# Gated values of two heads in units of one token tile by 512 columns, in a hybrid decoder trunk

## The chip, the cores and the metric

The kernel runs as one program on one core of a Trainium2 chip. The metric is the time of one execution in microseconds of device time; lower is better. Before the change the median of three runs is 835.55 us (834.86 to 836.42 us).

## The reference, cut to what matters

One layer of a decoder works on 512 tokens of width 1024. After an RMS norm, one projection `h @ w_in` with 11352 columns makes the inputs of three branches: chunked gated linear attention (GLA, 4 heads), sparse attention with a top-k indexer (DSA, 8 query heads) and cross-attention into 256 memory tokens. Each branch is gated, projected and merged, and a last projection and norm close the layer. The change touches the GLA values `gv`: 1024 of the 11352 columns, 256 for each of four heads.

```python
h = rmsnorm(x, g_pre[i])
(gq, gk, gv, ga, gz, dq, dk, dv, iq, ik, iw, dz, xq, xz, gates) = split_cols(h @ w_in[i])
...
att = jnp.einsum('bnthd,bnshd->bnhts', q_d, k_d)
att = jnp.where(causal, att, jnp.zeros_like(att))
o_intra = jnp.einsum('bnhts,bnshv->bnthv', att, v)
def step(state, inp):
    qc, kc, vc, dc = inp
    o = jnp.einsum('bthd,bhdv->bthv', qc, state)
    state = dc[..., None] * state + jnp.einsum('bthd,bthv->bhdv', kc, vc)
    return state, o
...
o = o_intra + o_inter.transpose(1, 0, 2, 3, 4)
o = rmsnorm(o.reshape(B, L, H, dv), g_head)
return o.reshape(B, L, H * dv) * jax.nn.silu(z)
```

## The kernel before, in words

Every product of two float32 matrices is made of three matmuls on a high and a low part of each operand: high by high, high by low, low by high (`mm3`, lines 106 to 109). The high part is a copy by ACT that rounds (`high`, line 94), the low part what is left, taken by DVE (`low`, lines 98 and 100).

Weights come from memory in loads of 1 MB, two chunks in each, into two buffers (`load_next`, L130). A chunk of 1024 columns on 128 partitions is split into its parts `whi` and `wlo` (`split_next`), which have four buffers each. The high part is issued at once; the low part is put on the list `late` and issued by `flush`, which runs behind the matmuls of the next quarter. When the last chunk of a load is split, the next load is issued on SP's queue.

The work is a list of units, in an order written out by hand. A unit is an accumulator of 128 by 512 in PSUM (tag `mm`, two buffers), filled in four quarters by 24 or 48 matmuls and then evicted by its `done`. Unit u needs chunk u (a pair of value units shares two chunks). In the main loop (from line 1103) each quarter's matmuls are issued, then `flush`, then `need`, which splits chunks up to an index ahead of time, then `done` after the fourth quarter, and then whatever `at(name, s, ...)` has hung on this slot. Slots count on beyond a unit's own four: `at("gz1.0", 11, ...)` runs eleven quarters after the first of `gz1.0`. Every engine works through its own instructions in this order.

The units begin with `dv` (0 and 1, in an opening of their own), `pc` (2), `gv0.0`, `gv0.1`, `gv1.0`, `gv1.1` (3 to 6), `iq0` and `iq1` (7 to 10), and then for each GLA head `gqk` (two units), for heads 2 and 3 `gv` (two units), and `gz` (two). In this order `gqk2` are units 19 and 20 and `gv2` units 21 and 22.

A `gv` unit (`unit_n`) takes two token tiles of 128 tokens by one head's 256 columns: the tokens are the stationary operand, the weights the moving one, in 48 matmuls of 256 columns. The values of heads 0 and 1 are made from the input before its norm is known (`g_lhs`), so their eviction multiplies by `rstd`, one 256-column piece at a time (`gv_done`); those of heads 2 and 3 use the normalised input and are evicted in one piece of 512.

On the slots behind `pc` hang the steps that finish the norm (`h_norm`, nine of them), `gate_operands`, the evictions of the four `dv` accumulators (`dv_done`) and the gates' logarithms (`gate_log`). On those behind `gz` hang attention, state, output, norm and result of each GLA head (`gla_att`, `gla_turn_k`, `gla_state`, `gla_out`, `gla_norm`, `gla_y`) and sixteen rounds of top-k (`topk_max`, `topk_drop`), which begin at `gz1.0`.

Of the kernel before, what the change touches and what calls it, by code (L numbers as in the profile page):

```python
# [11 lines left out]
F32R = mybir.dt.float32r  # L12
# [8 lines left out]
KT = 8  # L21
# [4 lines left out]
OFF = {}  # L26
# [15 lines left out]
    _pair(f"iq{_i}", OFF["iq"] + 256 * _i, OFF["iq"] + 256 * _i + 128)  # L42
for _h in range(4):
    _pair(f"gqk{_h}", OFF["gq"] + 128 * _h, OFF["gk"] + 128 * _h)
    for _n in ("gv", "gz", "dq", "dz", "xq", "xz"):
        _pair(f"{_n}{_h}", OFF[_n] + 256 * _h, OFF[_n] + 256 * _h + 128)
_pair("dk", OFF["dk"], OFF["dk"] + 128)
_pair("dv", OFF["dv"], OFF["dv"] + 128)
for _b in range(3):
    for _j in range(4):  # L50
        _c = OFF["gates"] + 1024 * _b + 256 * _j
        _pair(f"gate{_b}{_j}", _c, _c + 128)
NORMAL = ("gv", "dv")
PIDX = {n: i for i, (n, _, _) in enumerate(PAIRS)}


@with_exitstack
def trunk(ctx, tc, x, x_t, mem, w_in, w_c, w_kv, w_out, w_o, cols, g_mem, g_post, w_up, toe, out):
    nc = tc.nc
    pe, act, dve, pool, sp = nc.tensor, nc.scalar, nc.vector, nc.gpsimd, nc.sync  # L60

# [19 lines left out]
    def w4(name, dt=F32, n=1024):  # L81
        return wk.tile([128, n], dt, name=name, tag="w4", bufs=6)
# [19 lines left out]
    def split(hi, lo, src, scale=1.0):  # L102
        high(hi, src, scale)
        low(lo, src, hi, scale)

    def mm3(o, lh, ll, rh, rl, first=True, last=True):
        pe.matmul(o, lh, rh, start=first, stop=False)  # L107
        pe.matmul(o, lh, rl, start=False, stop=False)  # L108
        pe.matmul(o, ll, rh, start=False, stop=last)  # L109


    chunks, loads = [], []
# [54 lines left out]
    units, slots = [], {}  # L167
    where = {}

    def unit(name, quarter, done):  # L170
        where[name] = len(units)
        units.append((quarter, done))

    def at(name, s, fn, *a):
        slots.setdefault(4 * where[name] + s, []).append((fn, a))
# [16 lines left out]
    def unit_n(name, first, lhs, tiles, done):  # L192

        o = []

        def quarter(q):
            if q == 0:
                o.append(psum("mm", name))
            n = len(tiles)
            for i in range(2 * n * q, 2 * n * q + 2 * n):  # L200
                j, k = divmod(i, KT)
                wh, wl = chunks[first + k // 4][3]
                ah, al = lhs(k, tiles[j])
                mm3(o[0][:, 256 * j:256 * j + 256], ah, al, wh[:, k % 4], wl[:, k % 4],
                    k == 0, k == KT - 1)

        unit(name, quarter, lambda: done(o[0]))

    hh = keep.tile([128, KT, T], F32R, name="hh", tag="hh")
    hl = keep.tile([128, KT, T], F32R, name="hl", tag="hl")  # L210
# [23 lines left out]
    def win_n(name, done, lhs=h_lhs):  # L234
        add_chunks(w_in[PIDX[name]], True)
        first = len(units)
        for i in range(2):
            unit_n(f"{name}.{i}", first, lhs, (2 * i, 2 * i + 1), lambda p, i=i: done(i, p))
# [61 lines left out]
    R = {}  # L300

    def dv_done(tt, p):
        if tt == 0:
            R["dvh"], R["dvl"] = kv4("dvh", [4, 256], F32R), kv4("dvl", [4, 256], F32R)
        split(R["dvh"][:, tt], R["dvl"][:, tt], p[:, :256], R["rstd"][:, tt:tt + 1])
# [66 lines left out]

    GV = {}

    def gv_done(h, i, p):
        if i == 0:
            GV[h] = [w4(n, F32R).rearrange("p (t d) -> p t d", t=4) for n in ("vh", "vl")]
        vh, vl = GV[h]
        if h < 2:
            for j in range(2):  # L380
                tt = 2 * i + j
                split(vh[:, tt], vl[:, tt], p[:, 256 * j:256 * j + 256], R["rstd"][:, tt:tt + 1])
            return
        split(vh[:, 2 * i:2 * i + 2], vl[:, 2 * i:2 * i + 2], p.rearrange("p (t d) -> p t d", t=2))

    for h in range(2):
        win_n(f"gv{h}", lambda i, p, h=h: gv_done(h, i, p), g_lhs)


    def gate_log(h):  # L390
# [23 lines left out]

    at("pc", 0, rstd_row)
    for tt in range(4):
        at("gv1.0", tt, lambda tt=tt: dv_done(tt, R["dvps"][tt]))
    for k in range(9):
        at("pc", 1 + k, h_norm, k)

# [13 lines left out]

    for i in range(2):
        win_t(f"iq{i}", iq_done, n=384, rhs=lambda k: (hh[:, k, 128:512], hl[:, k, 128:512]))
    at("gv0.1", 2, gate_operands)
    at("iq0.1", 2, turn_iw)
    for h in range(4):
        at("gv1.1", h, gate_log, h)  # L440
    at("iq0.0", 3, gate_ln, 0)
    at("iq0.1", 0, gate_ln, 1)

# [157 lines left out]

    def gla_state(h, p):
        g = G[h]
        vh, vl = GV[h]
        kv = psum("at", "kv")
        mm3(kv[:, :256], g["kkh"][:, 128 * p:128 * p + 128], g["kkl"][:, 128 * p:128 * p + 128],
            vh[:, p], vl[:, p])
        S = w2("S", n=256)
        if p == 0:
            act.activation(S, kv[:, :256], AF.Copy)  # L610
        else:
            dve.scalar_tensor_tensor(S, g["Sp"], g["pd"][:, p:p + 1], kv[:, :256],
                                     op0=OP.mult, op1=OP.add)
        sh = w2("Sh", F32R)
        split(sh[:, 0:256], sh[:, 256:512], S)
        g["Sp"] = S
        g["S"].append(sh)

    def gla_out(h, i):
        g = G[h]  # L620
        vh, vl = GV[h]
        if i == 0:
            g["on"] = w4("on")
        on = g["on"]
        po = psum("at", "po")
        ss = s8("gss", 2)
        for j in range(2):
            p = 2 * i + j
            o = po[:, 256 * j:256 * j + 256]
            mm3(o, g["ah"][:, p], g["al"][:, p], vh[:, p], vl[:, p], True, p == 0)  # L630
            if p:
                s, sh = slice(128 * p - 128, 128 * p), g["S"][p]
                mm3(o, g["q2h"][:, s], g["q2l"][:, s], sh[:, 0:256], sh[:, 256:512], False, True)
        for j in range(2):
            p = 2 * i + j
            act.activation(on[:, 256 * p:256 * p + 256], po[:, 256 * j:256 * j + 256],
                           AF.Square, scale=1.0 / 16, accum_out=ss[:, j:j + 1])
        v = s8("gvar", 2)
        pool.tensor_scalar(v, ss, EPS, None, op0=OP.add)
        g["r", i] = po, rstd_of(v, 2)  # L640
# [18 lines left out]

    for h in range(4):  # L660
        win_t(f"gqk{h}", lambda i, p, h=h: (gla_q, gla_k)[i](h, p))
        if h > 1:
            win_n(f"gv{h}", lambda i, p, h=h: gv_done(h, i, p))
        z_units(f"gz{h}")


# [317 lines left out]
    def split_b(i):  # L984
        split_next([w[:, i].rearrange("p (k m) -> p k m", m=512) for w in F["w"]])


    for i in range(24):
        at("gqk0.0", 2+i, score, 1 + i // 8, i % 8)
# [4 lines left out]
        at(f"gz{h - 1}.1", 0, gla_exps, h)  # L994
    for h in range(4):
        z = f"gz{h}"
        if h < 2:
            at(z + ".0", h, gla_att, h, 0)
            at(z + ".0", h + 1, gla_att, h, 1)
            at(z + ".0", h + 2, gla_turn_k, h)  # L1000
            for p in range(3):
                at(z + ".1", 2*p + h, gla_state, h, p)
            after = 6 + h
        else:
            v = f"gv{h}"
            at(v + ".1", 0, gla_att, h, 0)
            at(v + ".1", 1, gla_att, h, 1)
            at(v + ".1", 2, gla_turn_k, h)
            for p in range(3):
                at(z + ".0", 2+p, gla_state, h, p)  # L1010
            after = 2
        for i in range(2):
            at(z + ".1", after + 2 * i, gla_out, h, i)
            at(z + ".1", after + 2 * i + 1, gla_norm, h, i)
            at(z + ".1", after + 10 + 2 * i, gla_y, h, i)
# [35 lines left out]
    with tc.manual_schedule():  # L1051
# [3 lines left out]
        loads[0][2] = wdv  # L1055
        state["load"] = 1
        act.dma_start(col, cols)
        for k in range(2):
            act.dma_start(R["xt"][0][:, k], x_t[:, k])
        for k in range(4):  # L1060
            h, c = k // 2, slice(512 * (k % 2), 512 * (k % 2) + 512)
            sp.dma_start(wdv[:, h, c], loads[0][0][:, h, c])
            if k:
                sp.dma_start(R["xt"][k], x_t[:, 2 * k:2 * k + 2])
        for tt in range(4):
            sp.dma_start(xs[tt], x[128 * tt:128 * tt + 128])
            if tt == 1:
                load_next()
# [34 lines left out]
        for u in range(2, len(units)):  # L1103
            quarter, done = units[u]
            for s in range(4):
                quarter(s)
                flush()
                if s == 1 and u < wo_first:
                    need(u + 2)
                if s == 3 and u + 2 < wo_first and chunks[u + 2][2]:  # L1110
                    need(u + 3)
                if s == 2 and u == wo_first - 1 or s == 0 and u == wo_first:
                    need(u + 3, True)
                if s == 3:
                    done()
                for fn, a in slots.pop(4 * u + s, []):
                    fn(*a)
# [12 lines left out]
def _layout(inputs):  # L1130
# [20 lines left out]
    wc[:, 64:80] = w[:, OFF["ga"]:OFF["ga"] + 16]  # L1151
    wc[:, 80:88] = w[:, OFF["iw"]:OFF["iw"] + 8]
    wc[:, 96:112] = wc[:, 64:80]
    a["w_c"] = pairs(wc, [(0,)])[0]
    four = [(256 * j, 256 * j + 128) for j in range(4)]
    wkv = np.asarray(inputs["w_mem_kv"])[0]
# [34 lines left out]
```

## Time and profile before

| | before |
|---|---|
| median of three runs | 835.55 us |
| the profiled execution's own time | 835.18 us |
| its span | 833.5 us |
| PE busy | 818.7 us, 98% |
| DVE busy | 473.8 us, 57% |
| ACT busy | 337.1 us, 40% |
| GpSimd busy | 50.2 us, 6% |
| HBM over the span | 101 GB/s |

Times inside the profile count from the start of the span, and the profiled execution takes 1.7 us more than its span. PE is TensorE's matmuls, DVE is VectorE, ACT is ScalarE, POOL is GpSimd and SP the engine whose queue issues most transfers. A matmul's duration contains its way through the array; successive ones overlap, so their cost is read from start to start. `Lnn` is a line of the kernel; `high`, `low` and `mm3` are helpers, so lines 94, 98, 100 and 107 to 109 are told apart by the tiles that they write. In square brackets a row may say how long the engine stood idle before the instruction and what ended that.

### The profile page before, as it was taken

The numbers are of one execution on the slowest core, as the hardware profiler recorded it, in microseconds if no ns is written. First come the engines' busy times: TensorE is split into PE (matmuls) and PEld (weight loads), VectorE is DVE, ScalarE is ACT, GpSimd is POOL, SyncE is SP. The second block draws the span as 40 slices with busy tenths as digits, with TensorE's granted clock in tenths as the row PEclk, the third lists the DMA queues.
The fourth block names the chain that finished last, engine by engine and source line by source line (L and its number), as shares of the span: only waits on it lengthen the run. The fifth ranks groups of instructions, "written<-read, shape, count | busy, mean of one in ns | idle before, by whom it ended". The sixth has DMA issues, their size and how long they took to land.

```text
span 833.5 us, 10783 instructions
## 1 busy us (share of the span) xinstructions
PE 818.7 (98%) x4320; PEld 704.3 (85%) x4320; DVE 473.8 (57%) x850; ACT 337.1 (40%) x608; POOL 50.2 (6%) x74
## 2 busy tenths in 40 slices
PE   7989999999999999999999999999999999999997
PEld 7989888989888888888888888889989898888885
DVE  4759677888686435446676543545655554343623
ACT  6577554453423223334444422334434343322320
POOL 1000010010000030032131000000000000000000
PEclk9999999999999999999999999999999999999999
DMA  9324121121222231222131125323324142226402
GB/s 332 117 102 138 51 91 62 52 101 53 100 101 101 101 105 73 101 104 99 51 108 71 51 101 176 101 101 101 112 92 147 56 152 70 86 98 223 156 1 102
DMA packets 16387, 86.30 MB, mean 104 GB/s; under 512 B 2064, under 2 KB 2576, under 8 KB 7760
## 3 DMA queue, kind: packets, MB, share of 16 engines
q1 hardware_dynamic: 15328, 84.02, 28.6%
q10 hardware_dynamic: 1008, 1.58, 0.5%
q8 instruction: 34, 0.56, 0.3%
q14 instruction: 17, 0.14, 0.0%
HBM read 82.42 MB, written 2.10 MB: 101 GB/s over the span
## 4 chain that ended last, share of the span: by engine, by line
PE 86%; DVE 5%; ACT 4%; DMA 2%; issue 2%; ACTq 0%; SPq 0%; DVEq 0%; POOLq 0%; POOL 0%
PE out L109 5%; PE out L107 5%; PE out L108 5%; PE pfin L109 2%; PE pfin L108 2%; PE pfin L107 2%; DVE wlo L98 1%; DMA x<-x 1%; PE tpp L721 1%; ACT whi L94 1%; DMA xt<-x_t 1%; PE pov L108 1%; PE pov L109 1%; PE lg L109 1%; PE lg L108 1%
## 5 line engine op out<-in xcount | busy, mean ns | idle before, releaser
L98 DVE TENSOR_TENSOR wlo<-wraw,whi 128x1024 fp32r<-128x1024 f32 (+1 forms) x135 | 163.4, 1211 | 84.4 <-ACT whi L94 83.5
L94 ACT ACTIVATE whi<-wraw 128x1024 fp32r<-128x1024 f32 (+1 forms) x135 | 139.4, 1039 | 22.2 <-PE out L108 19.6
L107 PE MATMUL out<-yh,whi 128*128 128x512 f32 x192 | 75.3, 392 | 0.0
L109 PE MATMUL out<-yh,wlo 128*128 128x512 f32 x192 | 74.8, 390 | 0.0
L108 PE MATMUL out<-yl,whi 128*128 128x512 f32 x192 | 74.8, 389 | 0.0
L707 ACT ACTIVATE bm<-bm,nm 128x128 f32<-128x128 f32 (+3 forms) x32 | 18.0, 564 | 73.6 <-DVE nm L705 71.8
L691 POOL TENSOR_TENSOR bm<-toe,madd 128x128 f32<-128x128 f32 (+3 forms) x32 | 31.0, 986 | 194.6 <-DMA toe<-toe 86.3
L109 PEld LDWEIGHTS out<-yh,wlo 128*128 128x128 f32 x192 | 36.0, 188 | 7.5
L107 PEld LDWEIGHTS out<-yh,whi 128*128 128x128 f32 x192 | 36.1, 188 | 7.3
L108 PEld LDWEIGHTS out<-yl,whi 128*128 128x128 f32 x192 | 36.1, 188 | 7.2
L94 ACT ACTIVATE yh<-th 128x512 fp32r<-128x512 f32 x16 | 10.1, 632 | 44.0 <-DVE th L657 24.9
L512 DVE SCALAR_TENSOR_TENSOR gth<-gth,out 128x512 f32<-128x512 f32 x16 | 11.0, 686 | 28.0 <-PE out L109 28.0
L273 POOL TENSOR_TENSOR rstd<-var,mhalf 128x1 f32<-128x1 f32 x6 | 3.3, 550 | 374.9 <-DVE var L952 289.7
L470 DVE MATCH_REPLACE8 madd<-m,madd 128x256 f32<-128x256 f32 (+2 forms) x48 | 25.6, 543 | 0.0
L466 DVE MAX8 m<-madd 128x8 f32<-128x256 f32 (+2 forms) x48 | 23.6, 546 | 0.0
L705 DVE CUSTOM_DVE_ANT_0 bm<-lg,bm 128x128 f32<-128x128 f32 (+3 forms) x32 | 15.5, 486 | 12.9 <-PE lg L109 12.7
L751 DVE TENSOR_TENSOR ydsa<-pov,th 128x128 f32<-128x128 f32 x32 | 7.8, 286 | 22.5 <-PE pov L109 22.1
L94 ACT ACTIVATE pth<-tpp 128x128 fp32r<-128x128 f32 (+3 forms) x32 | 13.7, 428 | 13.4 <-PE tpp L721 13.4
L456 DVE SCALAR_TENSOR_TENSOR madd<-relu,iw,madd 128x256 f32<-128x256 f32 (+2 forms) x21 | 12.9, 616 | 9.2 <-ACT relu L452 8.9
L949 ACT ACTIVATE sq<-pfin 128x512 f32<-128x512 f32 x8 | 4.8, 598 | 31.5 <-PE pfin L109 31.5
L98 DVE TENSOR_TENSOR yl<-th,yh 128x512 fp32r<-128x512 f32 x16 | 11.1, 693 | 11.2 <-ACT yh L94 11.2
L98 DVE TENSOR_TENSOR ptl<-tpp,pth 128x128 fp32r<-128x128 f32 (+3 forms) x32 | 15.5, 484 | 0.0
(1024 smaller groups left out, 2359.1 us busy)
## 6 DMA issues: line engine op xcount, KB each, us to landing
wraw<-w_in SPq DMA_DIRECT2D x43, 1024.0 KB, 4.8
wraw<-w_out SPq DMA_DIRECT2D x12, 1024.0 KB, 4.8
wraw<-w_kv SPq DMA_DIRECT2D x8, 1024.0 KB, 4.8
wraw<-w_o SPq DMA_DIRECT2D x4, 1024.0 KB, 4.8
x<-x SPq DMA_DIRECT2D x4, 512.0 KB, 8.2
toe<-toe SPq DMA_DIRECT2D x8, 256.0 KB, 5.2
xres<-x SPq DMA_DIRECT2D x4, 512.0 KB, 8.5
xt<-x_t SPq DMA_DIRECT2D x3, 512.0 KB, 7.6
```

The lines of the kernel that those rows point to most:

```text
L94: act.activation(hi, src, AF.Copy, scale=scale)
L98: dve.tensor_tensor(lo, src, f(hi), op=OP.subtract)
L107: pe.matmul(o, lh, rh, start=first, stop=False)
L108: pe.matmul(o, lh, rl, start=False, stop=False)
L109: pe.matmul(o, ll, rh, start=False, stop=last)
L456: dve.scalar_tensor_tensor(sc, r[:, :n], iw[:, b, h:h + 1], sc, op0=OP.mult, op1=OP.add)
L466: dve.max(out=M8[b], in_=maskadd[b])
L470: dve.match_replace(out=maskadd[b], in_to_replace=M8[b], in_values=maskadd[b], imm_value=-FMAX)
L512: dve.scalar_tensor_tensor(th, th, 1.0, p, op0=OP.add, op1=OP.mult)
L691: pool.tensor_tensor(bm[:, :n], Q[hp]["toe"][i][:, 384 - 128 * qb:512], maskadd[qb], op=OP.add)
L705: dve.tensor_tensor_reduce(out=bm[:, :n], in0=lg[:, :n], in1=bm[:, :n], scale=-1.0, scalar=FMAX, op0=OP.add, op1=OP.min, accum_out=nm)
L707: act.activation(bm[:, :n], bm[:, :n], AF.Exp, scale=-1.0, bias=nm, accum_out=su)
```

## The change

The four pairs of value units become two groups of four wide units, `gvw0` (heads 0 and 1, units 3 to 6) and `gvw1` (heads 2 and 3, units 21 to 24). A wide unit (`wide_units`) takes one token tile by 512 columns, which are two heads, in 24 matmuls; quarter q uses the group's chunk q, so each unit of a group uses all four chunks. The weights have a layout of their own, `w_gv`. The value tiles hold two token tiles by 512 columns; `gv_of` cuts out a head's part.

The order of splits is now `ahead`: in front of a group, chunk f+1 is split in the second and f+2 in the fourth quarter of unit f-1, and f+3 behind the first quarter of unit f; no further chunk is split until the group's last unit, which orders the next two. With head 3 losing its own value units, its GLA steps hang on `gz3` as those of heads 0 and 1 do. In the opening, one transfer of `x_t` goes from ACT's queue to SP's, behind the first piece of `wdv`; `dv_done` and `gate_operands` move to slots in `gvw0.2` and `gvw0.3`.

```diff
-    for _n in ("gv", "gz", "dq", "dz", "xq", "xz"):
+    for _n in ("gz", "dq", "dz", "xq", "xz"):
...
+    wide = set()
+
+    def wide_units(name, src, lhs, done):
+
+        first = len(units)
+        wide.add(first)
+        for i in range(2):
+            add_chunks(src[i], None)
+        for tt in range(4):
+            o = []
+
+            def quarter(q, tt=tt, o=o):
+                if q == 0:
+                    o.append(psum("mm", name))
+                wh, wl = chunks[first + q][3]
+                for k in (2 * q, 2 * q + 1):
+                    ah, al = lhs(k, tt)
+                    mm3(o[0], ah, al, wh[:, k % 2], wl[:, k % 2], k == 0, k == KT - 1)
+
+            unit(f"{name}.{tt}", quarter, lambda tt=tt, o=o: done(tt, o[0]))
...
-    def gv_done(h, i, p):
-        if i == 0:
-            GV[h] = [w4(n, F32R).rearrange("p (t d) -> p t d", t=4) for n in ("vh", "vl")]
-        vh, vl = GV[h]
-        if h < 2:
-            for j in range(2):
-                tt = 2 * i + j
-                split(vh[:, tt], vl[:, tt], p[:, 256 * j:256 * j + 256], R["rstd"][:, tt:tt + 1])
-            return
-        split(vh[:, 2 * i:2 * i + 2], vl[:, 2 * i:2 * i + 2], p.rearrange("p (t d) -> p t d", t=2))
-
-    for h in range(2):
-        win_n(f"gv{h}", lambda i, p, h=h: gv_done(h, i, p), g_lhs)
+    def gv_done(g, tt, p):
+        if tt == 0:
+            GV[g] = [[w4(n, F32R).rearrange("p (t d) -> p t d", t=2) for n in ("vh", "vl")]
+                     for _ in range(2)]
+        vh, vl = GV[g][tt // 2]
+        split(vh[:, tt % 2], vl[:, tt % 2], p, 1.0 if g else R["rstd"][:, tt:tt + 1])
+
+    def gv_of(h, p):
+        return [t[:, p % 2, 256 * (h % 2):256 * (h % 2) + 256] for t in GV[h // 2][p // 2]]
+
+    wide_units("gvw0", [w_gv[0], w_gv[1]], g_lhs, lambda tt, p: gv_done(0, tt, p))
...
-        at("gv1.0", tt, lambda tt=tt: dv_done(tt, R["dvps"][tt]))
+        at("gvw0.2", 1 + tt, lambda tt=tt: dv_done(tt, R["dvps"][tt]))
...
-    at("gv0.1", 2, gate_operands)
+    at("gvw0.2", 0, gate_operands)
...
-        at("gv1.1", h, gate_log, h)
+        at("gvw0.3", h, gate_log, h)
...
-        if h > 1:
-            win_n(f"gv{h}", lambda i, p, h=h: gv_done(h, i, p))
+        if h == 2:
+            wide_units("gvw1", [w_gv[2], w_gv[3]], h_lhs, lambda tt, p: gv_done(1, tt, p))
...
+    def ahead(u, s):
+
+        f = max([w for w in wide if w <= u], default=-9)
+        if u <= f + 2:
+            if (u, s) == (f, 0):
+                need(f + 3)
+        elif u == f + 3:
+            if s < 2:
+                need(f + 4 + s)
+        else:
+            if s == 1:
+                need(u + 2)
+            if s == 3 and (u + 1 in wide or u + 2 < wo_first and chunks[u + 2][2]):
+                need(u + 3)
...
-        if h < 2:
-            at(z + ".0", h, gla_att, h, 0)
-            at(z + ".0", h + 1, gla_att, h, 1)
-            at(z + ".0", h + 2, gla_turn_k, h)
+        if h != 2:
+            d = int(h > 0)
+            at(z + ".0", d, gla_att, h, 0)
+            at(z + ".0", d + 1, gla_att, h, 1)
+            at(z + ".0", d + 2, gla_turn_k, h)
             for p in range(3):
-                at(z + ".1", 2*p + h, gla_state, h, p)
-            after = 6 + h
+                at(z + ".1", 2 * p + d, gla_state, h, p)
+            after = 6 + d
...
-        for k in range(2):
-            act.dma_start(R["xt"][0][:, k], x_t[:, k])
+        act.dma_start(R["xt"][0][:, 0], x_t[:, 0])
         for k in range(4):
             h, c = k // 2, slice(512 * (k % 2), 512 * (k % 2) + 512)
             sp.dma_start(wdv[:, h, c], loads[0][0][:, h, c])
             if k:
                 sp.dma_start(R["xt"][k], x_t[:, 2 * k:2 * k + 2])
+            else:
+                sp.dma_start(R["xt"][0][:, 1], x_t[:, 1])
...
-                if s == 1 and u < wo_first:
-                    need(u + 2)
-                if s == 3 and u + 2 < wo_first and chunks[u + 2][2]:
-                    need(u + 3)
+                if u < wo_first:
+                    ahead(u, s)
...
+    gv = w[:, OFF["gv"]:OFF["gv"] + 1024].reshape(2, 2, 2, 128, 2, 512)
+    a["w_gv"] = np.ascontiguousarray(gv.transpose(4, 0, 3, 1, 2, 5).reshape(4, 128, 2, 1024))
```

## Rows read from the trace of the kernel before

**Rows 1.** The page: busy time, share and instructions by engine.
```profile
PE 818.7 (98%) x4320; PEld 704.3 (85%) x4320; DVE 473.8 (57%) x850; ACT 337.1 (40%) x608; POOL 50.2 (6%) x74
```
**Rows 2.** The page: the chain that ended last, by engine.
```profile
PE 86%; DVE 5%; ACT 4%; DMA 2%; issue 2%; ACTq 0%; SPq 0%; DVEq 0%; POOLq 0%; POOL 0%
```
**Rows 3.** Waits of PE, whole span: waiter, releaser, us in total, times, longest.
```profile
PE gv1.1_587 L107 <- DVE vl L100: 2.5, 1, 2.5
...
PE gv1.0_521 L108 <- DVE wlo L98: 0.6, 1, 0.6
...
PE po L107 <- ACT relu L452: 0.4, 1, 0.4
```
**Rows 4.** Busy us by stretch: length, PE, PEld, DVE, ACT, POOL, clock, DMA, GB/s.
```profile
46.80:57.69 10.89, 8.42 (x54) 8.07 (x53) 6.04 (x11) 8.54 (x18) 0.00 (x0) 0.84 0.01 2
...
125.00:152.00 27.00, 27.00 (x147) 22.77 (x146) 20.44 (x42) 12.59 (x25) 2.04 (x3) 1.00 0.14 49
```
**Rows 5.** Matmuls by tile: count, duration ns min/median/max, first and last start us.
```profile
L107 PE MATMUL gv0.1_452<-whi,gh x16: 283/283/283, 34.4 to 39.8; 128*128 128x256 f32 x16
L107 PE MATMUL pfin<-whi,mgh x32: 389/389/389, 783.7 to 804.8; 128*128 128x512 f32 x32
```
**Rows 6.** Timeline of PE at the last value unit: start us, us, instruction.
```profile
49.39 0.48 PE L107 MATMUL gv1.1_587<-whi,gh 128*128 128x256 f32 x1 [2.47 <-DVE vl L100]
...
51.80 0.41 PE L109 MATMUL gv1.1_587<-whi,gl 128*128 128x256 f32 x1
```
**Rows 7.** Timeline of ACT, early: chunk 5's high part, a norm step, an eviction.
```profile
27.41 1.06 ACT L94 ACTIVATE whi<-wraw 128x1024 fp32r<-128x1024 f32 x1 [0.62 <-DMA wraw<-w_in]
...
31.36 0.62 ACT L94 ACTIVATE hh<-xt 128x512 fp32r<-128x512 f32 x1
...
59.80 0.47 ACT L94 ACTIVATE vh<-gv1.1_587,rstd 128x256 fp32r<-128x256 f32 x1 [0.55 <-DVE vl L100]
```
**Rows 8.** Timeline of DVE, early: chunk 5's low part, a norm step, an eviction.
```profile
33.35 1.21 DVE L98 TENSOR_TENSOR wlo<-wraw,whi 128x1024 fp32r<-128x1024 f32 x1
...
35.15 0.68 DVE L98 TENSOR_TENSOR hl<-xt,hh 128x512 fp32r<-128x512 f32 x1
...
69.89 0.56 DVE L98 TENSOR_TENSOR iql<-iq0.1_711,iqo 64x384 fp32r<-64x384 f32 x1
```
**Rows 9.** Timeline of PE in the opening: the second four matmuls of `dv`.
```profile
9.38 0.74 PE L315 MATMUL dvps<-whi,gh 128*128 128x256 f32 x4 [1.32 <-ACT gh L94]
```
**Rows 10.** Timeline of PE: first matmuls of the units `iq0.0` and `iq1.1`.
```profile
57.69 0.34 PE L107 MATMUL iq0.0_672<-hh,whi 128*128 128x384 f32 x1
...
70.79 0.33 PE L107 MATMUL iq1.1_802<-hh,whi 128*128 128x384 f32 x1
```
**Rows 11.** Timeline of ACT before the second group: the norms of head 1.
```profile
152.14 0.84 ACT L647 ACTIVATE on<-po,rstd 128x256 f32<-128x256 f32 x2 [1.13 <-POOL rstd L273]
...
154.84 0.84 ACT L647 ACTIVATE on<-po,rstd 128x256 f32<-128x256 f32 x2 [1.12 <-POOL rstd L273]
```
**Rows 12.** Timeline of DVE before the second group: last of a top-k round, max8, `gla_k`.
```profile
151.78 0.68 DVE L470 MATCH_REPLACE8 madd<-m,madd 128x512 f32<-128x512 f32 x1
...
153.51 1.48 DVE L466 MAX8 m<-madd 128x8 f32<-128x256 f32 x3
...
156.08 0.35 DVE L569 TENSOR_TENSOR kk<-kte,eb 128x192 f32<-128x192 f32 x1
```
**Rows 13.** Timeline of PE: behind unit 20's second quarter; first of units 21, 22.
```profile
148.03 0.28 PE L107 MATMUL po<-vh,ah 128*128 128x256 f32 x1
...
152.21 0.28 PE L107 MATMUL gv2.0_1615<-whi,hh 128*128 128x256 f32 x1
...
157.95 0.28 PE L107 MATMUL gv2.1_1672<-whi,hh 128*128 128x256 f32 x1
```
**Rows 14.** Timeline of all engines: the last square of x, and the start of `pc`.
```profile
19.19 1.06 ACT L1096 ACTIVATE x<-x 128x1024 f32<-128x1024 f32 x1 [0.59 <-DMA x<-x]
...
21.34 0.50 PE L107 MATMUL pc<-gh,whi 128*128 128x512 f32 x1
```

More of the change, by code (lines that the diff above doesn't have):

```diff
@@ L52, with trunk @@
         _pair(f"gate{_b}{_j}", _c, _c + 128)
-NORMAL = ("gv", "dv")
+NORMAL = ("dv",)
 PIDX = {n: i for i, (n, _, _) in enumerate(PAIRS)}
 @with_exitstack
-def trunk(ctx, tc, x, x_t, mem, w_in, w_c, w_kv, w_out, w_o, cols, g_mem, g_post, w_up, toe, out):
+def trunk(ctx, tc, x, x_t, mem, w_in, w_gv, w_c, w_kv, w_out, w_o, cols, g_mem, g_post, w_up, toe, out):
     nc = tc.nc
@@ L603, in gla_state @@
         g = G[h]
-        vh, vl = GV[h]
+        vh, vl = gv_of(h, p)
         kv = psum("at", "kv")
         mm3(kv[:, :256], g["kkh"][:, 128 * p:128 * p + 128], g["kkl"][:, 128 * p:128 * p + 128],
-            vh[:, p], vl[:, p])
+            vh, vl)
         S = w2("S", n=256)
@@ L620, in gla_out @@
         g = G[h]
-        vh, vl = GV[h]
         if i == 0:
@@ L629, in gla_out @@
             o = po[:, 256 * j:256 * j + 256]
-            mm3(o, g["ah"][:, p], g["al"][:, p], vh[:, p], vl[:, p], True, p == 0)
+            mm3(o, g["ah"][:, p], g["al"][:, p], *gv_of(h, p), True, p == 0)
             if p:
@@ L996, in trunk @@
         z = f"gz{h}"
-        if h < 2:
-            at(z + ".0", h, gla_att, h, 0)
-            at(z + ".0", h + 1, gla_att, h, 1)
-            at(z + ".0", h + 2, gla_turn_k, h)
+        if h != 2:
[3 more added lines that the diff above has]
+            at(z + ".0", d + 2, gla_turn_k, h)
             for p in range(3):
-                at(z + ".1", 2*p + h, gla_state, h, p)
-            after = 6 + h
-        else:
[L1005 to L1008, printed above, removed]
+                at(z + ".1", 2 * p + d, gla_state, h, p)
+            after = 6 + d
+        else:
+            at("gvw1.1", 0, gla_att, h, 0)
+            at("gvw1.1", 1, gla_att, h, 1)
+            at("gvw1.1", 2, gla_turn_k, h)
             for p in range(3):
```

## The prediction, made before the result was known

> **What bounds the kernel now.** I read the page first. TensorE (PE) is busy 98% of the span, VectorE (DVE) 57%, ScalarE (ACT) 40% [rows 1], and the chain that ended last runs on PE for 86% of the span [rows 2]. So the question is what PE's stream costs, and where it stands still. The list of waits of PE answers the second part: the value units of the first two heads hold waits of 2.5 us and 0.6 us, and behind the first 80 us the longest entry is 0.4 us in total [rows 3]. PE is thus a dense stream there: a microsecond by which it is shorter comes back whole, and any new wait is paid whole. Third, the busy time by stage says whether the helpers have room: in 125 to 152 us PE is busy 27.00 of 27.00 us at the full clock, DVE 20.44 [rows 4]. That is where the second group of units goes, and DVE runs there with a backlog, as its timeline will show.
>
> Units and chunks are counted from zero as the loop does. The first wide group is units 3 to 6, the second units 21 to 24. Before, a group's third chunk was read two units after its first; now the first unit f reads chunk f+q in quarter q.
>
> **Part 1, the matmuls.** Removed: 384 matmuls of 256 columns. Added: 192 of 512. The first come every 120 ns (45 starts between 34.4 and 39.8 us), the second kind, as in the last projection, every 227 ns (93 starts between 783.7 and 804.8 us) [rows 5]. A unit goes from 48 x 0.120 = 5.74 us to 24 x 0.227 = 5.45 us: 0.29 us, and 2.3 us over eight units. The Trainium skill prices this lower: TensorE: Matmul & The Clock Gate, section Back-to-back issue gap, gives N/2.4 + 2.5 ns from start to start, so two matmuls of 256 columns would cost 2.5 ns more than one of 512, and 192 pairs 0.5 us as an estimate from that page. The trace disagrees (2 x 120 against 227 ns), and the rows decide.
>
> **Part 2, the first group.** It runs from 28.66 us (the 34.4 us of `gv0.1` [rows 5] less 48 x 0.120) to 57.69 us. What goes: the wait of 0.6 us for a low part, and the wait of 2.5 us for a free accumulator, whose eviction sat behind normalisation work [rows 3]. After that wait eleven periods from 49.39 to 51.80 us take 219 ns each instead of 120 [rows 6]: the lower of the two levels, 1.2 instead of 2.4 GHz. The mean granted clock over 46.80 to 57.69 us is 0.84 [rows 4], so 0.16 x 10.89 = 1.7 us were lost, in 3.5 us at half pace. With the four units' 4 x 0.29 = 1.2 us some 6.0 us could go here.
>
> What comes: the first wide unit needs chunk 5 in its third and chunk 6 in its fourth quarter. Its first two quarters and one matmul end at 28.66 + 13 x 0.227 = 31.6 us. The one after reads the low part of chunk 5. Nothing ahead of that part on ACT or DVE has moved: ACT still waits for the transfer until 27.41 us, and DVE still makes this low part at 33.35 us, for 1.21 us, behind the pc eviction and a normalisation [rows 7, 8]. So PE stands from 31.6 to 34.6 us: 2.9 us, new. Chunk 6 is ordered one slot later: its high part follows the ACT row at 31.36 us, and its low part follows the DVE pair that ended at about 35.8 us, so it is there at 36.9 us [rows 7, 8]. What does the clock do? The solid wait of 2.5 us brought it down [rows 6]; a wait of 1.32 us in the opening did not: the four matmuls behind it span 0.74 us, where at 219 ns a period they would take over 1 us [rows 9]. A solid 2.9 us is nearer the first, so I take the lower level for about 3.5 us. Then five matmuls at 0.43 us reach 36.7 us, the fourth quarter meets no further wait, and the unit ends at 38.7 us (38.1 with the clock held and a second wait of 1.0 us). Three units more at 5.45 us, and the four gate matmuls of 512 columns at the same 0.23 us, bring the iq stage to 56.0 us (55.4), against 57.69 us [rows 10]: 1.7 to 2.3 us earlier.
>
> Does that stay? The iq stage leans on DVE: the last read of one accumulator ended at 70.45 us, and the unit that reuses it began at 70.79 us [rows 8, 10], a slack of 0.3 us. ACT and DVE themselves gain from one eviction instead of two (two of 0.47 us with a wait of 0.55 between [rows 7], so 0.8 us) and from moving `gate_operands` and the `dv` evictions to where they are idle; but the high part of chunk 7 now waits until the last wide unit is past its first quarter, since it takes chunk 3's buffer, and the `dv` eviction and the gate logs stand behind it on ACT. That leaves them 1.3 to 1.8 us ahead. I take 1.5 us earlier for the group; the ends are 2.3 us earlier and, should the helpers pass on nothing, nothing.
>
> **Part 3, the second group (from 152.21 us).** DVE and ACT lag behind PE here. At the slot behind unit 20's second quarter PE is at 148.03 us [rows 13]; ACT, which must first do the norm of head 1, waiting for GpSimd, is free at 152.9 us [rows 11]. There the high part of chunk 22 now stands; before, it was ordered a half unit sooner, and its low part ran on DVE right after the row at 151.78 us, from 152.38 us [rows 12]. So the high part ends at 153.9 us and the low part at 155.2 us, DVE idling about 1.5 us meanwhile. Then DVE does what it did from 153.51 to 156.43 us (the max8 triple and the four products of `gla_k`, 2.9 us [rows 12]) and is free at 158.0 us; ACT's second norm moves from 154.84 us [rows 11] to 155.8 us, chunk 23's high part to 157.5 us, chunk 24's to 158.5 us. Low parts: chunk 23 at 159.2 us, chunk 24 at 160.4 us.
>
> PE: first quarter to 153.6 us; one matmul at 153.9, the rest of the quarter from 155.2 to 156.4 us; one matmul at 157.5, the rest from 159.3 to 160.4 us; the last quarter to 161.8 us. Before, unit 21 ended at 157.95 us [rows 13]. That is 3.8 us later. The three units behind it save 3 x 0.29 = 0.9 us. Net: 2.95 us lost. All of this rides on the clock of group one (if PE and helpers both come 1.5 us earlier, the relative times hold). The idle pieces here (0.3, 1.0, 1.1, 1.5 us) are nearer to the case that held its clock [rows 9], so I add nothing; a fall would add about 1.7 us [rows 6].
>
> **Part 4, the rest.** The transfer of x_t moved from ACT's queue to SP's may let the `dv` stage begin sooner, but `pc` starts at 21.34 us because the last square waits for x (19.19 us) and the weight's high part follows it [rows 14]; the bytes ahead of x are the same. Cost and gain nothing, 0.3 us either way at most. On SP the moved issue stands ahead of three pieces of `wdv`, and the same stage end hides it. For head 3 the `gla` steps move behind its first z unit: same instructions, no value tile is reused before it is read, and its y is due only at the first output unit, several units on. A matmul there that came too early would show as a wait of PE on `kd`; the 0.4 us of [rows 3] is the size of such a wait here, and I add nothing for it. Loads keep their order and their distance to the splits; I price them at nothing, and one that came late would show as ACT waiting for it, as the 0.62 us of [rows 7].
>
> **Sum.** -1.5 + 2.95 = +1.45 us on the profiled execution's 835.18 us: 836.6 us. The median of the runs is 0.37 us above that execution, so 837.0 us. About 0.2% (1.7 us) is what a measurement of this kernel can tell from no change, so the forecast lies inside, at the slow edge.
>
> **Rivals.**
> A. The clock also falls in the second group: +1.7 us, 838.7 us. For it: PE does seven matmuls, 1.6 us, between 153.6 and 159.3 us. Against: no idle piece over 1.6 us. It shows in the pace behind the second wait: 0.43 us a matmul.
> B. Faster: the helpers lose their lag at 148 us. If ACT reaches chunk 22's high part less than half a unit after PE passed its slot, all four chunks are there, and the second group saves 4 x 0.29 = 1.2 us; with 2.3 us from the first the time is 835.55 - 3.5 = 832.0 us. It decides itself at the norm of head 1: it must start before 149 us, against 152.14 us now [rows 11]. For it: DVE has 24% idle time around [rows 4], and evictions in group one are fewer. Against: nothing in that chain is removed.
> C. The change leaves no mark: the first wait is shorter because the `dv` stage ends sooner and all behind it with it, and the second costs about what the first gives: 835.5 us.
> D. Matmuls of 512 columns with tokens as weights take two periods of 120 ns: part 1 is lost, +2.3 us, 839.3 us. Against it: the last projection has the same form and takes 227 ns [rows 5]. By the Trainium skill's formula (TensorE: Matmul & The Clock Gate, section Back-to-back issue gap) 1.8 of these 2.3 us would be lost, and the time would be 838.8 us as an estimate from that page.
>
> **How the numbers follow.** Forecast 0.40 (836.0 to 838.0 us), A 0.20, B 0.22, C 0.15, D 0.03. Faster by over 0.2%: B, 0.22. Slower by over 0.2%: A, D and the upper part of the forecast's own range, 0.38. Within: 0.40. The range that leaves out two in ten cuts the better half of B and the tail of A and D: 832.6 to 839.2 us.
>
> **What would show it.** Right: a wait of about 2.9 us in the first unit of group one on a low part of DVE, none on an accumulator in its last unit, the iq stage at 56 us; in the first unit of group two two waits of 1 to 3 us on low parts, its end near 160 us (161.8 less what group one gave). Wrong: no wait in unit 21, or an iq stage later than 57.7 us. The pace should be 227 ns in all eight units, as in [rows 5].

## The result, and the profile after

| | before | after |
|---|---|---|
| median, five runs each on one chip | 835.34 us (834.86 to 836.42) | 840.02 us (839.09 to 841.80) |
| the profiled execution, its span, its mean granted clock | 835.18, 833.5 us, 0.997 | 839.09, 837.4 us, 0.999 |

The kernel after takes 1.0059 [1.0048, 1.0071] times as long: 0.6% slower, where I had forecast 837.0 us and no measurable change. The profiled execution is the fastest of the five.

First the page of after: busy time by engine and the chain that ended last, for [rows 1, 2].

```profile
PE 816.8 (98%) x4128; PEld 692.2 (83%) x4128; DVE 473.8 (57%) x846; ACT 337.2 (40%) x604; POOL 49.8 (6%) x74
...
PE 82%; DVE 8%; ACT 4%; issue 2%; DMA 2%; SPq 0%; POOL 0%; DVEq 0%; POOLq 0%; ACTq 0%
```

PE is busy 1.9 us less and the span is 3.9 us longer. The chain says where to look: its share on PE fell from 86 to 82%, its share on DVE rose from 5 to 8%. PE's waits in after (waiter, releaser, us in total, times, longest), for [rows 3]:

```profile
PE gvw L108 <- DVE wlo L98: 5.1, 4, 2.8
...
PE kv L109 <- DVE kkl L98: 1.5, 1, 1.5
PE gvw L107 <- ACT whi L94: 1.5, 2, 1.3
...
PE pc L107 <- ACT whi L94: 1.1, 1, 1.1
```

The waits on an accumulator and on `gv1.0`'s low part (2.5 and 0.6 us) are gone. In their place the wide units wait 6.6 us for weights, and a GLA state matmul waits 1.5 us. To place them, PE's timeline of after (start us, us, instruction, idle before) in the first group, for [rows 6, 10, 14]:

```profile
21.33 0.50 PE L107 MATMUL pc<-gh,whi 128*128 128x512 f32 x1 [1.09 <-ACT whi L94]
...
28.64 0.39 PE L107 MATMUL gvw<-whi,gh 128*128 128x512 f32 x1
...
31.36 0.39 PE L107 MATMUL gvw<-whi,gh 128*128 128x512 f32 x1
34.59 0.50 PE L108 MATMUL gvw<-wlo,gh 128*128 128x512 f32 x1 [2.85 <-DVE wlo L98]
...
36.99 0.50 PE L108 MATMUL gvw<-wlo,gh 128*128 128x512 f32 x1 [0.74 <-DVE wlo L98]
...
38.26 0.39 PE L107 MATMUL gvw<-whi,gh 128*128 128x512 f32 x1
...
55.49 0.33 PE L107 MATMUL iq0.0_568<-hh,whi 128*128 128x384 f32 x1
```

The matmuls from 28.64 to 31.36 us are twelve periods of 227 ns. Unit 3 stands at its 14th matmul, the first to read chunk 5's low part, and ends at 38.26 us; `iq0.0` comes at 55.49 us, 2.20 us earlier than in [rows 10]. In the second group, for [rows 13]:

```profile
150.57 0.39 PE L107 MATMUL gvw<-whi,hh 128*128 128x512 f32 x1
...
152.35 0.50 PE L107 MATMUL gvw<-whi,hh 128*128 128x512 f32 x1 [0.26 <-ACT whi L94]
153.61 0.50 PE L108 MATMUL gvw<-wlo,hh 128*128 128x512 f32 x1 [0.76 <-DVE wlo L98]
...
156.29 0.50 PE L107 MATMUL gvw<-whi,hh 128*128 128x512 f32 x1 [1.26 <-ACT whi L94]
157.59 0.51 PE L108 MATMUL gvw<-wlo,hh 128*128 128x512 f32 x1 [0.80 <-DVE wlo L98]
...
160.22 0.39 PE L107 MATMUL gvw<-whi,hh 128*128 128x512 f32 x1
...
218.83 0.39 PE L109 MATMUL kv<-vh,kkl 128*128 128x256 f32 x1 [1.54 <-DVE kkl L98]
```

Unit 21 takes 9.65 us instead of 5.74. What ACT did meanwhile, for [rows 11]:

```profile
150.51 0.84 ACT L665 ACTIVATE on<-po,rstd 128x256 f32<-128x256 f32 x2 [1.13 <-POOL rstd L294]
151.24 1.06 ACT L94 ACTIVATE whi<-wraw 128x1024 fp32r<-128x1024 f32 x1
...
154.46 0.84 ACT L665 ACTIVATE on<-po,rstd 128x256 f32<-128x256 f32 x2 [1.43 <-POOL rstd L294]
155.19 2.00 ACT L94 ACTIVATE whi<-wraw 128x1024 fp32r<-128x1024 f32 x2
```

And DVE, in the second group, for [rows 12], and at head 3's state:

```profile
152.33 1.23 DVE L98 TENSOR_TENSOR wlo<-wraw,whi 128x1024 fp32r<-128x1024 f32 x1 [1.50 <-ACT whi L94]
153.47 1.48 DVE L485 MAX8 m<-madd 128x8 f32<-128x256 f32 x3
...
156.32 2.35 DVE L98 TENSOR_TENSOR wlo<-wraw,whi 128x1024 fp32r<-128x1024 f32 x2
...
216.25 1.47 DVE L485 MAX8 m<-madd 128x8 f32<-128x256 f32 x3
217.64 0.67 DVE L509 SCALAR_TENSOR_TENSOR th<-th,gz3.0_1950 128x512 f32<-128x512 f32 x1
218.23 0.55 DVE L98 TENSOR_TENSOR kkl<-tk,kkh 128x384 fp32r<-128x384 f32 x1
```

Between PE's need and the part that answers it, both helpers do other work: ACT the norms of head 1, DVE a max8 triple of the top-k and, at head 3's state, a z gate.

An account by stage makes the loss plain. From the first matmuls of `pc`, `iq0.0`, `gqk2.1`, `gz2.0`, `gate00.0` and `pfin` in the timelines, the stretches in us (lower is better; before's `gv3` lies in its fourth stretch):

```
              group one  iq..gqk2.1  group two   heads 2, 3  the rest
              pc-iq0.0               gqk2.1-gz2  -gate00.0   -pfin
before          36.35      87.59           110.09            528.33
after           34.16      88.16       36.26      78.81      528.29
g2_early        36.54      88.14       33.05      78.81      528.30
g1_early        29.95      88.14       36.25      78.83      528.30
h3_later        36.58      88.14       37.79      77.01      528.27
all_three       31.50      88.13       33.03      77.01      528.31
dma_back        33.80      88.13       36.29      78.81      528.27
fill            34.15      88.14       36.26      78.83      528.29
all3_fill       29.96      88.15       33.03      77.01      528.23
```

After gains 2.19 us in group one, gives 0.57 back in the iq stage and loses 36.26 + 78.81 - 110.09 = 4.98 us behind it. Those make 3.36 us; the last 0.6 us is the stretch from `pfin` to the end (49.8 us before, 50.4 after). It arises behind the issue of the last output transfer (833.46 - 830.47 = 2.99 us before, 837.37 - 833.78 = 3.59 after). Over all kernels here the stretch lies between 49.8 and 50.9 us; whether it belongs to the kernel or to the execution, one profile of each cannot tell.

The 4.98 us can be split by tile, adding up PE's matmuls from start to start between `gqk2.1` and `gate00.0`. The value units take 26.48 us instead of 23.70, 2.8 us more; the state products `kv` take 3.92 instead of 2.12, 1.8 us more; all others together 0.4 us more.

The five executions of after also differ, and with the mean clock granted to each:

```
clock   0.999   0.995   0.995   0.993   0.991
us     839.09  839.89  840.02  841.24  841.80
```

### The profile page after: what moved, and what is told of

The parts are those of the page before. It is cut to its first block, busy times and chain, and to the rows that moved or that the text cites. A ratio compares the mean times of both kernels' runs of the same rounds, so it can differ in the third digit from the quotient of the medians.

```text
span 837.4 us, 10381 instructions
## 1 busy us (share of the span) xinstructions
PE 816.8 (98%) x4128; PEld 692.2 (83%) x4128; DVE 473.8 (57%) x846; ACT 337.2 (40%) x604; POOL 49.8 (6%) x74
## 4 chain that ended last, share of the span: by engine, by line
PE 82%; DVE 8%; ACT 4%; issue 2%; DMA 2%; SPq 0%; POOL 0%; DVEq 0%; POOLq 0%; ACTq 0%
PE out L109 5%; PE out L108 5%; PE out L107 5%; DVE wlo L98 2%; PE pfin L109 2%; PE pfin L108 2%; PE pfin L107 2%; PE gvw L108 1%; PE gvw L109 1%; PE gvw L107 1%; DMA x<-x 1%; ACT whi L94 1%; PE tpp L739 1%; DMA wraw<-w_in 1%; DVE m L485 1%
## 5 line engine op out<-in xcount | busy, mean ns | idle before, releaser
L108 PE MATMUL gvw<-wlo,gh 128*128 128x512 f32 x32 | 12.7, 396 | 3.6 <-DVE wlo L98 3.6
```

## The experiments

My theory: the value units lose to three places where a helper delivers late (unit 3's low parts, unit 21's parts, head 3's `kkl`), and to the clock falling at those waits in some executions. The rivals: the wide form itself costs the time; moving orders only moves the wait; the clock excess comes from the moved transfer. Each experiment edits the kernel after unless said otherwise, and all are timed over five rounds against the kernel before on the same chip. Ratios are to before. After itself was not timed again beside them; before's medians in these timings lie between 835.34 and 835.48 us, so differences to after's 840.02 us hold to some tenths of a microsecond.

**g2_early**: the orders of chunks 22, 23 and 24 come two, three and three quarters earlier, behind the last quarter of unit 19 and the first two of unit 20.

```diff
+        elif u == 20:
+            if s < 2:
+                need(23 + s)
         else:
...
-            if s == 3 and (u + 1 in wide or ...):
+            if s == 3 and (u == 19 or u + 1 in wide or ...):
```

> Changed kernel, with the four splits of the second wide group ordered earlier: chunks 21 to 24 behind the second and fourth quarter of unit 19 and behind the first and second of unit 20. The waits theory (PE is a dense stream, its 3.1 us of waits in unit 21 are paid whole because the high part of chunk 22 stands behind head 1's norm on ACT) expects the four waits of unit 21 to shrink below 0.5 us in total, the units behind to begin about 3 us earlier, and about 837.0 us against the changed kernel's 840.0. The backlog theory (DVE is the local bound from 130 to 160 us, so a wait removed in unit 21 comes back in units 22 to 26 or at head 3) expects under 1 us of gain, 839 to 840 us, with new waits of 2 us or more further on.

Measured: 836.40 us, 1.0016 [1.0007, 1.0025]. Unit 21's four waits go, one of 0.7 us comes at the start of unit 22, and the stretch of group two falls from 36.26 to 33.05 us. So 3.2 us of after's loss is this order; the wide units are not slow themselves. Group one is 2.4 us longer than after's in this profile although nothing there was edited. PE's timeline of g2_early shows why:

```profile
36.44 0.50 PE L108 MATMUL gvw<-wlo,gh 128*128 128x512 f32 x1 [2.86 <-DVE wlo L98]
36.78 0.40 PE L109 MATMUL gvw<-whi,gl 128*128 128x512 f32 x1
37.01 0.53 PE L107 MATMUL gvw<-whi,gh 128*128 128x512 f32 x1
37.34 0.63 PE L108 MATMUL gvw<-wlo,gh 128*128 128x512 f32 x1
37.77 0.63 PE L109 MATMUL gvw<-whi,gl 128*128 128x512 f32 x1
```

Behind the same wait (2.86 us against 2.85) these matmuls come every 0.43 us, the lower level, where after's kept 0.23. The units 3 to 6 take 27.62 us against 26.85: 0.77 us. Another fall, in `pc`, stretches that from 7.31 to 8.92 us.

**g1_early**: chunk 6's high part is ordered with the last quarter of `pc`, and the waiting low parts go right behind the first instruction of `pc`'s eviction, ahead of the normalisation.

```diff
         dve.tensor_tensor(p, o, R["row"], op=OP.mult)
+        flush()
...
+            if (u, s) == (2, 3):
+                need(6)
```

> Changed kernel, with chunk 6 of the first wide group ordered one slot earlier and both low parts of chunks 5 and 6 issued on DVE right behind the first operation of the pc eviction, where DVE stood idle for 1.9 us. The waits theory expects the 2.85 and 0.74 us in unit 3 to go, the iq stage to begin at 51.4 to 52 us instead of 55.5, and, if the helpers keep up, 836.0 us; the chain of gate logs on ACT may keep one microsecond of it, 837 us. The backlog theory expects the gain to be given back inside the iq stage, where DVE has a slack of 0.3 us: iq1.1 with a wait of 2 us or more, 839 us.

Measured: 837.36 us, 1.0022 [1.0013, 1.0031]; the profiled execution 835.65 us at clock 0.998. DVE's timeline of g1_early has both low parts at once, 3.6 us earlier than [rows 8] for the first:

```profile
29.12 0.69 DVE L358 TENSOR_TENSOR pc<-pc,row 128x512 f32<-128x512 f32 x1
29.73 2.35 DVE L98 TENSOR_TENSOR wlo<-wraw,whi 128x1024 fp32r<-128x1024 f32 x2
```

No wait is left in unit 3 and group one takes 29.95 us: 4.2 us less than after, all of it kept to `pfin` but for the 0.3 us by which `pc` starts later. The iq stage takes 88.14 us as in after, so the normalisation that was pushed back costs nothing that shows, and the backlog theory fails. The profiled execution is the fastest of eleven, though: the median is only 2.7 us under after's.

**h3_later**: head 3's state steps, and what follows them, two slots later.

```diff
-                at(z + ".1", 2 * p + d, gla_state, h, p)
-            after = 6 + d
+                at(z + ".1", 2 * p + d + 2 * (h == 3), gla_state, h, p)
+            after = 6 + d + 2 * (h == 3)
```

> Changed kernel, with head 3's states and outputs hung two slots later, so that the low part of the turned keys (kkl) is ready when the first state product needs it. The waits theory, which puts 1.5 us of the missed size on this wait, expects it gone and 838.5 us. Its rival (the missed size is the clock, which falls at the waits of the wide units in most executions and not in the profiled one) expects the wait gone from the profile as well, but PE to stand elsewhere in that stage, and 840.0 us.

Measured: 841.51 us, 1.0072 [1.0059, 1.0085], against my 838.5: a miss. The profile splits it. The wait for `kkl` is gone, as DVE's row and PE's of h3_later show, and the stretch of heads 2 and 3 takes 77.01 instead of 78.81 us, 1.8 us less.

```profile
222.49 0.55 DVE L98 TENSOR_TENSOR kkl<-tk,kkh 128x384 fp32r<-128x384 f32 x1
```
```profile
224.10 0.28 PE L109 MATMUL kv<-vh,kkl 128*128 128x256 f32 x1
```

But the clock fell at `pc`, in unit 3 and in unit 21; two of these in the view of busy time by stretch (PE, PEld, DVE, ACT, POOL, clock, DMA, GB/s), of h3_later:

```profile
31.00:42.00 11.00, 8.07 (x28) 5.73 (x27) 8.51 (x13) 5.84 (x10) 0.00 (x0) 0.84 0.50 159
...
155.00:165.00 10.00, 7.11 (x21) 4.99 (x22) 7.92 (x16) 3.84 (x10) 1.22 (x2) 0.83 0.53 193
```

and of after, where the first stretch holds the same wait in unit 3 and the second the last two waits of unit 21 (1.26 and 0.80 us; 1.25 and 0.81 in h3_later):

```profile
31.00:42.00 11.00, 7.42 (x32) 5.49 (x31) 10.54 (x16) 5.57 (x9) 0.00 (x0) 1.00 0.40 136
...
155.00:165.00 10.00, 7.95 (x42) 6.29 (x41) 7.71 (x17) 2.78 (x4) 0.00 (x0) 1.00 0.55 206
```

Group two is 1.53 us longer for it (37.79 against 36.26). This kernel's five executions have clocks of 0.988 to 0.992. Why an edit that acts from 217 us on goes with more falls ahead of it, no run settles.

**all_three**: the three edits together.

> All three edits together. The waits theory adds them: 840.0 - 3.0 - 4.0 - 1.5 = 831.5 us, faster than the kernel before by 0.4%, and, with no wait over 1 us left in the value units, a mean granted clock of at least 0.998 in every execution. The backlog theory expects 836 us or more. If the clock falls have another cause than the waits of the wide units, the spread of the executions stays near the 2.7 us of the changed kernel.

Measured: **830.25 us**, 0.9936 [0.9922, 0.9949]: 9.8 us faster than after and 5.2 us faster than before. The medians of the single edits came to -3.6, -2.7 and +1.5 us against after; together they give more than their sum. My reading, not shown by itself, is that each wait that goes takes a place with it where the clock could fall. The stretches do add: 33.03 and 77.01 us are those of g2_early and h3_later, while group one has 1.55 us over g1_early's 29.95 from a fall at `pc`. I had expected a clock of 0.998 or better in every execution; they were 0.996 to 0.999. DVE's row, and PE's only wait in group two, at the first matmul of unit 22, of all_three:

```profile
148.49 3.49 DVE L98 TENSOR_TENSOR wlo<-wraw,whi 128x1024 fp32r<-128x1024 f32 x3
```
```profile
154.60 0.50 PE L107 MATMUL gvw<-whi,hh 128*128 128x512 f32 x1 [0.67 <-DVE kk L588]
```

Three low parts stand ahead of the max8 triple; what is left is the accumulator that `gla_k` reads.

Against before, the whole gain is group one: 31.50 us for 36.35 (29.96 in all3_fill below). The iq stage costs 0.5 us more, and group two with the heads behind it gives nothing: 33.03 + 77.01 = 110.04 us against 110.09. There the value units' matmuls take 23.25 us with that wait, against 23.70, and the matmuls around them 0.4 us more than before.

**dma_back**: both first transfers of `x_t` on ACT's queue, as before.

```diff
-        act.dma_start(R["xt"][0][:, 0], x_t[:, 0])
+        for k in range(2):
+            act.dma_start(R["xt"][0][:, k], x_t[:, k])
...
-            else:
-                sp.dma_start(R["xt"][0][:, 1], x_t[:, 1])
```

> Changed kernel, with the moved transfer of x_t back on ACT's queue, so that the opening is as before. The clock theory (a part of the missed size is that the faster opening leaves PE standing 1.1 to 1.5 us before pc, that the clock falls there in most executions but not in the changed kernel's profiled one, and that pc then takes some 1.7 us longer) expects the wait before pc to be gone, pc at the full clock, and 1 to 1.6 us less than the changed kernel's 840.0: 838.4 to 839.0 us. The view of the prediction (this move costs and gains nothing) expects 840.0 us within 0.5.

Measured: 840.04 us, 1.0069 [1.0053, 1.0084], no change to after. The clock theory's 838.4 to 839.0 us failed. The wait of 1.1 us at `pc` goes and the opening waits grow: the first row, of dma_back, has the clock at 0.88, the second, of after, at 1.00, and `pc` starts at 22.67 instead of 21.33 us.

```profile
7.00:21.30 14.30, 12.25 (x85) 11.76 (x86) 7.57 (x15) 11.29 (x19) 0.74 (x1) 0.88 1.01 380
```
```profile
7.00:21.30 14.30, 12.10 (x96) 11.53 (x95) 7.50 (x14) 11.43 (x19) 0.68 (x1) 1.00 1.00 386
```

So the transfer is not the cause of the excess; with it back, a wait and a fall in the opening stand in place of the wait at `pc`.

**fill**: matmuls into an accumulator that nobody reads, where PE stands; the arithmetic is otherwise after's.

```diff
+        fills = {(2, 0): 5, (3, 2): 12, (3, 3): 4, (21, 1): 4, (21, 2): 8}
...
+                    for i in range(fills[u, s]):
+                        pe.matmul(sc, l[:, 0:128], r, start=True, stop=True)
```

> Changed kernel, with matmuls whose result nobody reads put where PE would stand: 5 before pc, 12 and 4 before the third and fourth quarter of unit 3, 4 and 8 before the second and third of unit 21, about as long as the waits there. They add work (33 matmuls of 512 columns, 7.5 us at the full pace) and take nothing else away. The clock theory expects every execution to keep its clock in these places, hence a time at or a little under the changed kernel's fastest, 838.5 to 839.5 us, a mean granted clock of 0.998 or more and a spread under 1.5 us. If the excess over the fastest execution has another cause than the clock, the time stays at 840 us or rises with the added work by up to 2 us.

Measured: 839.54 us, 1.0051 [1.0039, 1.0063]; 839.45 to 840.25, clocks 0.997 and 0.998, so time and clock lie just outside what the clock theory expected. The stretches are after's to 0.02 us, so the added matmuls took only idle time past `pc`, and the median comes to 0.45 us above the profiled execution of after instead of 0.93, with `pc` itself starting 0.59 us later (21.92 against 21.33; 21.64 in g1_early and 21.77 in all_three, without such matmuls). The spread falls from 2.7 to 0.8 us. This supports the reading that the spread of after is the clock falling at its waits.

**one_only**: heads 2 and 3 as before; group one wide, with the opening and the moved steps.

```diff
+    for _n in ("gv",) * (_h > 1) + ("gz", "dq", "dz", "xq", "xz"):
...
+        if h > 1:
+            win_n(f"gv{h}", lambda i, p, h=h: gv_old(h, i, p))
```

> Only the first wide group (heads 0 and 1) and the moves of the opening; heads 2 and 3 have their own value units and their old slots as before. The account by parts (first group 1.6 us earlier at the full clock; second group +2.95 us net; head 3's slots +1.5 to 2.2 us; falls of the clock at pc and in unit 3 up to 2.7 us more) expects 833.7 us where the clock holds and up to 836.5 us where it falls twice, median 835 us, and no difference to the kernel before but a constant shift from 76 us on. The prediction's own term for this part (-1.5 us) expects 834.0 us.

Measured: 835.03 us, 0.9999 [0.9990, 1.0007]. In its profile the clock fell in unit 3 (units 3 to 6 take 27.61 us) and `pc` came at 22.28 us, 0.94 later than before. The first group alone, as it stands, gives nothing that can be told from before; what it gives without its wait and without a second wide group was not run, but g1_early's stretch puts 4.2 us on that wait and its companion.

**best1**: all_three with dma_back.

> The three edits that took the waits away (830.25 us together), with the moved transfer back on ACT's queue. The clock theory expects the wait before pc (1.2 us) to go, no fall of the clock before pc or behind it, the executions within 1 us of each other, and 829.5 to 830.2 us; the prediction's view of that move expects no difference, 830.25 us with the same spread of 1.7 us.

Measured: 830.75 us, 0.9943 [0.9931, 0.9955]: no gain over all_three and outside the 829.5 to 830.2 of the clock theory, as dma_back foretells. The wait at `pc` is gone, and the clock fell in the opening (0.88 over 7 to 21.3 us).

**before_moved**: the kernel *before*, with only `gate_operands` and the `dv` evictions in later slots, as the change has them.

```diff
-        at("gv1.0", tt, lambda tt=tt: dv_done(tt, R["dvps"][tt]))
+        at("gv1.0", 1 + tt, lambda tt=tt: dv_done(tt, R["dvps"][tt]))
...
-    at("gv0.1", 2, gate_operands)
+    at("gv1.0", 0, gate_operands)
```

> The kernel before, with only two of the moves: the gate operands behind the first quarter of gv1.0 instead of the third of gv0.1, the dv evictions one slot later. No wide unit. If the 2.5 us wait for an accumulator came from the gate operands standing ahead of the eviction of gv0.1, that eviction ends about 2.6 us earlier, the wait falls under 0.5 us, the clock holds, and the time is 831.0 to 832.5 us. If the wide units are what took that wait away (half the evictions), the wait stays over 2 us, and so does the time, 835.4 us.

Measured: 834.18 us, 0.9985 [0.9976, 0.9994], between the two cases. PE's waits of before_moved:

```profile
PE pla L395 <- DVE dvl L100: 1.6, 1, 1.6
...
PE iq1.1_802 L107 <- DVE iql L98: 0.5, 1, 0.5
```

The accumulator's wait of 2.5 us [rows 3] becomes one of 1.6 us for an accumulator under `pla`; the clock holds there, and `iq0.0` comes 2.48 us earlier. Then the iq stage gives 1.3 us back to DVE's evictions (`gqk0.0` only 1.16 us earlier), and 1.1 us stays. These two moved lines are worth 0.15%, 1.2 us, without any wide unit. So a part of all_three's 5.2 us needs no wide unit; narrow units with all orders and moves at their best were not run, and what the wide form adds to them stays open.

**all3_fill**: all_three with the five unread matmuls ahead of `pc` alone.

> The three edits together, with five matmuls whose result nobody reads in front of pc, where PE stands 1.2 us. If the fall of the clock behind that wait makes what is left of the spread, all executions come to the fastest of the three edits, 829.6 to 830.2 us, with a spread under 0.6 us. If the falls only move into the dv stage, as they did with the transfer moved back, the median stays at 830.25 or rises to 830.8 us.

Measured: **830.01 us** (829.90 to 830.17), 0.9936 [0.9923, 0.9948], the fastest and the steadiest, as the clock theory expected. `pc`'s stretch has the clock at 1.00 in all3_fill, where all_three has 0.82:

```profile
21.30:31.00 9.70, 8.90 (x42) 7.09 (x42) 7.34 (x9) 6.59 (x9) 0.75 (x1) 1.00 0.50 177
```
```profile
21.30:31.00 9.70, 8.71 (x34) 7.13 (x35) 5.89 (x7) 4.85 (x7) 0.79 (x1) 0.82 0.35 122
```

## Why the prediction was wrong, step by step

The forecast of 837.0 us missed the median by 3.0 us, and the range by 0.8.

- **Part 1 held.** 227 ns a matmul: units 4 to 6 run from 38.26 to 55.49 us, 17.2 us, for 3 x 5.45 and four gate matmuls at 0.23. Rival D is out. The Trainium skill (TensorE: Matmul & The Clock Gate, section Back-to-back issue gap) gives its formula for the gap of an isolated matmul, 109 and 216 ns here. This case's trace has 120 and 227 ns, so that formula does not price this exchange. In group two the four units' 1.2 us were used up by the wait in unit 22 and the matmuls around (all_three).
- **Part 2 held in the profiled execution.** Predicted: a wait of 2.9 us at the low part of chunk 5, a second of 1.0, the unit's end at 38.1 us with the clock held; measured 2.85, 0.74 and 38.26 us. Net -1.63 us at `gqk2.1` (143.65 against 145.28 us) for -1.5. The prize of 6.0 us was sound: g1_early's group one is 6.4 us shorter than before's. The reason that I gave for the part handed back, helpers only 1.3 to 1.8 us ahead, is not borne out: the iq stage takes 88.12 to 88.16 us in every wide kernel, whether it begins at 51.59 us or at 58.24. That the net still came out near is in part luck. The fall that I expected in unit 3 did not come there, but with the same wait it came in the profiles of g2_early, h3_later, dma_back and one_only, for 0.55 to 0.82 us (units 3 to 6 against after's 26.85 us); I had 0.6.
- **Part 3 held.** Low part of chunk 22 at 155.2 less 1.6 us, measured 153.56; of chunk 23 at 157.6, when PE's matmul on it starts (157.59); the unit's end at 160.1 to 160.2, measured 160.22. The two waits on low parts read 0.76 and 0.80 us, under the 1 to 3 us that I had named as the sign: the row counts from the end of the matmul in flight, from start to start less one period they are 1.03 and 1.07. The value units lose 2.8 us for 2.95 (3.2 with the matmuls around them; g2_early takes 3.2 away). Rival B had the wrong switch: nothing in head 1's chain had to go, the orders had to come earlier. Nor did its prize of 1.2 us in group two come (110.04 against 110.09 us).
- **Part 4 failed: "I add nothing" for head 3.** It cost 1.8 us. I named the place and sized it by the 0.4 us of another wait [rows 3], and looked for a wait on `kd`. I did not write out what stands on DVE's queue at the new slots: the `kkl` of the first state step stands behind a max8 triple of 1.47 us and the z gate of 0.67. The products `kv` take the whole 1.8 us more than before, and h3_later and all_three get it back.
- **The clock: right prices, wrong use.** A fall costs 1.6 us at `pc`, some 0.8 in unit 3, 1.5 in unit 21 (rival A had 1.7). I chose one pattern of falls; each of these places falls in the profiles of some kernels and not of others. After's median lies 0.93 us above a profile without any, where before's lies 0.16 above its own; I carried over 0.37. That falls make this difference is what the five clocks and fill support, since the four other executions of after have no trace.
- **The end.** 0.6 us between `pfin` and the end of the span, behind the last transfer's issue; I had no term for it, and its cause stays open.

Sum of the misses: 1.8 for head 3, 0.6 at the end, 0.56 between execution and median (0.93 less 0.37), 0.06 in groups one and two and the matmuls around them: 3.0 us. The "cost and gain nothing" of Part 4 for the moved transfer is borne out by dma_back (840.04 against 840.02).

## What to carry to other kernels

Fewer and larger instructions paid here only when the operands arrived earlier too: the same wide units are 0.6% slower or 0.6% faster than before by the slots of a few orders. For every step that is moved to a new slot, write down what stands ahead of its first instruction on each engine, and price that queue, not the median wait of the old place. Where a dense TensorE stream has waits of a microsecond or more, take all of them out together before judging: h3_later made its own stretch 1.8 us shorter and came out 1.5 us slower, with falls at the waits that it had left.

## What the runs showed of the hardware

The same wait in the same place brought the granted clock down in the profile of one kernel and not in that of another: 2.85 us in unit 3 held it in after (clock 1.00 over 31 to 42 us), behind 2.86 us it was 0.84 over that stretch in g2_early; at `pc`, 1.4 us held it in g1_early, 1.2 us did not in all_three (0.82 over 21.3 to 31 us). The length of the wait alone does not decide, and what does stays open. Five unread matmuls in such a wait went with the clock at 1.00 there in the profiles of fill and all3_fill, and the spread is 1.7 us in all_three and 0.3 in all3_fill, which ran on another chip.
